# Softmax over rows of 512: the last chunk's last row loaded by GpSimd in two unequal DMAs

## The chip, the cores and the metric

One core of one Trainium2 chip. The metric is device time in microseconds (us), the median over executions. The kernel before takes 162.28 us (six runs, 162.11 to 162.43). The profiles are of single executions; their span is some 1.8 us shorter than the device time of the same execution.

## The reference

```python
x: (16, 1024, 512) float32
def reference(x):
    x_scaled = x / 0.5
    x_max = np.max(x_scaled, axis=-1, keepdims=True)
    exp_x = np.exp(x_scaled - x_max)
    return exp_x / np.sum(exp_x, axis=-1, keepdims=True)
```

The input has 33.55 MB, and so has the output. Everything has to cross the DMA engines once in each direction.

## The kernel before

The 16384 rows are cut into 8 chunks. A chunk is 128 partitions of 16 rows of 512 numbers, so 32 KB per partition and 4 MB in all. Six buffers hold the chunks; the seventh and eighth reuse the first two once these have been stored.

```python
    LOADS = [[(0, 4), (4, G)]] + [WHOLE] * 7
    BLOCKS = [[(0, 4), (4, 8), (8, G)]] + [WHOLE] * 6 + [[(0, 8), (8, G)]]
    STORES = [WHOLE] * 8
    BUFS = 6
# ...
        for lo, hi in LOADS[c]:                       # SyncE issues all loads
            nc.sync.dma_start(out=xt[:, lo:hi, :], in_=xr[c][:, lo:hi, :])
# ...
    # per block: maxima (VectorE), exponentials with row sums (ScalarE),
    # reciprocal and multiplication of 7 rows in 8 (VectorE), the rest (ScalarE), store
        nc.vector.tensor_reduce(negmax[:, 0:b], chunks[c][:, lo:hi, :], axis=AX, op=MAX, negate=True)
# ...
            nc.scalar.activation(out=row, in_=row, func=EXP, bias=biases[i][:, g : g + 1],
                                 scale=2.0, accum_out=sums[i][:, g : g + 1])
# ...
        nc.vector.tensor_mul(rows, rows, recips[i][:, 0:k].unsqueeze(2).broadcast_to((P, k, D)))
# ...
                nc.scalar.dma_start(out=outr[c][:, lo:hi, :], in_=chunks[c][:, lo:hi, :])
```

Of the kernel before, what the change touches and what calls it, by code (L numbers as in the profile page):

```python
# [1 line left out]

# [4 lines left out]


@with_exitstack
def kernel(  # L10
    ctx: ExitStack,
    tc: tile.TileContext,
    x: bass.AP,
    out: bass.AP,
):
    nc = tc.nc
    fp32 = mybir.dt.float32
    P = nc.NUM_PARTITIONS
    AX = mybir.AxisListType.X
    EXP = mybir.ActivationFunctionType.Exp  # L20
    COPY = mybir.ActivationFunctionType.Copy
    MAX = mybir.AluOpType.max

    D = x.shape[-1]
    xf = x.flatten_outer_dims()
    of = out.flatten_outer_dims()
    N = xf.shape[0]




    G = 16
    C = N // (P * G)
    assert C * P * G == N
    xr = xf.rearrange("(c p g) d -> c p g d", p=P, g=G)
    outr = of.rearrange("(c p g) d -> c p g d", p=P, g=G)
    WHOLE = [(0, G)]
    LOADS = [[(0, 4), (4, G)]] + [WHOLE] * 7
    BLOCKS = [[(0, 4), (4, 8), (8, G)]] + [WHOLE] * 6 + [[(0, 8), (8, G)]]
    STORES = [WHOLE] * 8  # L40
    BMAX = 16
    BUFS = 6

    data = ctx.enter_context(tc.tile_pool(name="data", bufs=BUFS))
    stats = ctx.enter_context(tc.tile_pool(name="stats", bufs=6))

    ctx.enter_context(tc.manual_schedule())


    warm = stats.tile([P, 1], fp32, name="warm", bufs=1)  # L50
    nc.vector.memset(warm, 0.0)  # L51
    nc.scalar.activation(out=warm, in_=warm, func=EXP)  # L52

    chunks = {}
    blocks = [(c, lo, hi) for c in range(C) for lo, hi in BLOCKS[c]]
    n = len(blocks)
    biases, sums, recips = {}, {}, {}

    def load(c):
        if c < BUFS:  # L60
            chunks[c] = data.tile([P, G, D], fp32, name="xt")
        else:
            chunks[c] = chunks[c - BUFS]
        xt = chunks[c]
        for lo, hi in LOADS[c]:
            nc.sync.dma_start(out=xt[:, lo:hi, :], in_=xr[c][:, lo:hi, :])  # L66

    def shift(i):
        c, lo, hi = blocks[i]
        if c not in chunks:  # L70
            load(c)
        b = hi - lo
        negmax = stats.tile([P, BMAX], fp32, name="negmax")
        nc.vector.tensor_reduce(  # L74
            negmax[:, 0:b], chunks[c][:, lo:hi, :], axis=AX, op=MAX, negate=True
        )
        biases[i] = stats.tile([P, BMAX], fp32, name="bias")
        nc.vector.tensor_scalar_mul(biases[i][:, 0:b], negmax[:, 0:b], 2.0)  # L78

    def exponentials(i, rows):  # L80
        c, lo, hi = blocks[i]
        if i not in sums:
            sums[i] = stats.tile([P, BMAX], fp32, name="sums")
        for g in rows:
            row = chunks[c][:, lo + g, :]
            nc.scalar.activation(  # L86
                out=row,
                in_=row,
                func=EXP,
                bias=biases[i][:, g : g + 1],  # L90
                scale=2.0,
                accum_out=sums[i][:, g : g + 1],
            )


    def scale_vector(i):
        c, lo, hi = blocks[i]
        b = hi - lo
        k = b - b // 8
        recips[i] = stats.tile([P, BMAX], fp32, name="recip")  # L100
        nc.vector.reciprocal(recips[i][:, 0:b], sums[i][:, 0:b])  # L101
        rows = chunks[c][:, lo : lo + k, :]
        nc.vector.tensor_mul(  # L103
            rows, rows, recips[i][:, 0:k].unsqueeze(2).broadcast_to((P, k, D))
        )

    def scale_scalar(i):
        c, lo, hi = blocks[i]
        b = hi - lo
        for g in range(b - b // 8, b):  # L110
            row = chunks[c][:, lo + g, :]
            nc.scalar.activation(  # L112
                out=row, in_=row, func=COPY, scale=recips[i][:, g : g + 1]
            )

    def store(i):
        c, _, end = blocks[i]
        for lo, hi in STORES[c]:
            if hi == end:
                nc.scalar.dma_start(  # L120
                    out=outr[c][:, lo:hi, :], in_=chunks[c][:, lo:hi, :]
                )

    shift(0)
    shift(1)

    def rows(i):
        c, lo, hi = blocks[i]
        cut = hi - lo - (2 if c == 1 else 0)
        return range(cut), range(cut, hi - lo)  # L130

    exponentials(0, rows(0)[0])
    for i in range(n):
        if i + 1 < n:
            exponentials(i + 1, rows(i + 1)[0])
        scale_vector(i)
        scale_scalar(i)
        if i + 2 < n:
            shift(i + 2)
        store(i)  # L140
        if i + 1 < n:
            exponentials(i + 1, rows(i + 1)[1])


# [1 line left out]
_INS = ['x']  # L146
_OUTS = [((16, 1024, 512), 'float32')]


# [23 lines left out]
```

## Time and profile before

A DMA is cut into packets, which sixteen DMA engines carry. When an engine is through with its share, it writes a completion count of 4 B to the DMA's semaphore, a counter; a DMA has landed when all sixteen have written.

| what | kernel before | from |
|---|---|---|
| device time | 162.28 us | median of six runs |
| span of the profiled execution | 160.26 us | profile |
| VectorE busy | 134.6 us, idle after 147.42 | page; chain of work |
| bytes moved | 67.13 MB, 431 GB/s from 2.5 to 148 us | transfers view |
| last data packet ends | 159.06 us, the other engines' by 158.51 | packet records |
| last completion count of the last store | 159.41 us | completion records |
| from that count to the end of the span ("the tail") | 0.85 us | difference |

The page's third part splits the transfers by queue. The columns are packets, megabytes, and the time of these packets as a share of sixteen engines' span:

```profile
q1 hardware_dynamic: 1296, 33.56, 49.4%
q10 hardware_dynamic: 1152, 33.55, 48.5%
q14 instruction: 2, 0.02, 0.0%
```

q1 has the loads, q10 the stores, q14 the fetches of instructions. Loads and stores together hold the engines for 97.9% of the span.

### The profile page before, as it was taken

The page shows a single profiled execution, that of the slowest core. Times are in us where ns is not written, and L with a number is a line of the kernel's source. Part 1 is how long each engine was busy: PE and PEld are TensorE (multiplying, and loading weights), DVE is VectorE, ACT ScalarE, POOL GpSimd, SP SyncE. Part 2 cuts the span into 40 slices and gives each one's busy share as a digit, 9 for nine tenths or more (in the row PEclk, how much of TensorE's full clock was granted, in tenths as well). Part 3 has the DMA queues.
Part 4 walks back from the last instruction along what each step waited for, and adds up shares of the span by engine and source line. Part 5 has one row for each costly group of instructions (what it writes and reads, how often), then busy time and mean ns, then how long its engine had stood idle before and what let it go on. Part 6 is the DMA issues. An engine that isn't in the chain of part 4 may idle for free.

```text
span 160.3 us, 402 instructions
## 1 busy us (share of the span) xinstructions
DVE 134.6 (84%) x45; ACT 102.2 (64%) x273; POOL 0.2 (0%) x4
## 2 busy tenths in 40 slices
DVE  0607999999999999999999999999999999957000
ACT  3071549069989972998199909991899891690000
POOL 0000000000000000000000000000000000000000
DMA  5999999999999999999999999999999999999993
GB/s 180 474 409 491 409 401 483 425 393 452 458 393 401 393 425 474 409 393 499 417 393 474 442 393 468 442 393 442 474 393 417 491 401 401 491 417 401 466 442 139
DMA packets 2450, 67.13 MB, mean 419 GB/s; under 512 B 272, under 2 KB 272, under 8 KB 272
## 3 DMA queue, kind: packets, MB, share of 16 engines
q1 hardware_dynamic: 1296, 33.56, 49.4%
q10 hardware_dynamic: 1152, 33.55, 48.5%
q14 instruction: 2, 0.02, 0.0%
HBM read 33.55 MB, written 33.55 MB: 419 GB/s over the span
## 4 chain that ended last, share of the span: by engine, by line
DVE 80%; DMA 7%; ACT 4%; issue 0%; SPq 0%
DVE negmax L74 42%; DVE xt L103 36%; DMA xt<-in_x_dram 7%; ACT xt L86 4%; DVE bias L78 1%; DVE recip L101 1%; SPq L66 0%
## 5 line engine op out<-in xcount | busy, mean ns | idle before, releaser
L86 ACT ACTIVATE xt<-xt,bias 128x512 f32<-128x512 f32 x128 | 90.4, 708 | 41.5 <-DVE bias L78 40.6
L74 DVE TENSOR_REDUCE negmax<-xt 128x16 f32<-128x8192 f32 (+2 forms) x11 | 69.9, 6353 | 9.5 <-DMA xt<-in_x_dram 9.5
L103 DVE TENSOR_TENSOR xt<-xt,recip 128x7168 f32<-128x7168 f32 (+2 forms) x11 | 62.0, 5637 | 0.4
L86 ACT ACTIVATION_READ_ACCUMULATOR xt<-xt,bias 128x1 f32 x128 | 23.9, 187 | 0.0
L112 ACT ACTIVATE xt<-xt,recip 128x512 f32<-128x512 f32 x15 | 9.9, 707 | 0.0
L101 DVE RECIPROCAL recip<-sums 128x16 f32<-128x16 f32 (+2 forms) x11 | 2.4, 218 | 1.8 <-ACT xt L86 1.8
L78 DVE TENSOR_SCALAR bias<-negmax 128x16 f32<-128x16 f32 (+2 forms) x11 | 1.9, 173 | 0.4
L52 ACT ACT_TABLE_LOAD x1 | 1.3, 1283 | 0.7 <-PEq L157 0.7
L51 DVE MEMSET warm<- 128x1 f32 x1 | 0.1, 59 | 0.8 <-PEq L157 0.8
L52 ACT ACTIVATE warm<-warm 128x1 f32<-128x1 f32 x1 | 0.2, 202 | 0.0
L157 POOL MEMSET const-bfloat16-1.0<- 128x1 bf16 x1 | 0.1, 101 | 0.0
L157 POOL MEMSET const-uint8-127<- 128x1 uint8 x1 | 0.1, 101 | 0.0
L157 POOL MEMSET const-float32-0.0<- 128x1 f32 x1 | 0.1, 98 | 0.2 <-issue 0.2
L157 POOL MEMSET const-float32-1.0<- 128x1 f32 x1 | 0.1, 98 | 0.0
## 6 DMA issues: line engine op xcount, KB each, us to landing
out_dram<-xt ACTq DMA_DIRECT2D x8, 4096.0 KB, 22.8
xt<-in_x_dram SPq DMA_DIRECT2D x7, 4096.0 KB, 30.1
xt<-in_x_dram SPq DMA_DIRECT2D x1, 3072.0 KB, 11.7
xt<-in_x_dram SPq DMA_DIRECT2D x1, 1024.0 KB, 4.8
```

What stands on the lines that cost most here:

```text
L51: nc.vector.memset(warm, 0.0)
L52: nc.scalar.activation(out=warm, in_=warm, func=EXP)
L74: nc.vector.tensor_reduce(negmax[:, 0:b], chunks[c][:, lo:hi, :], axis=AX, op=MAX, negate=True)
L78: nc.vector.tensor_scalar_mul(biases[i][:, 0:b], negmax[:, 0:b], 2.0)
L86: nc.scalar.activation(out=row, in_=row, func=EXP, bias=biases[i][:, g : g + 1], scale=2.0, accum_out=sums[i][:, g : g + 1],)
L101: nc.vector.reciprocal(recips[i][:, 0:b], sums[i][:, 0:b])
L103: nc.vector.tensor_mul(rows, rows, recips[i][:, 0:k].unsqueeze(2).broadcast_to((P, k, D)))
L112: nc.scalar.activation(out=row, in_=row, func=COPY, scale=recips[i][:, g : g + 1])
L157: nc = _bacc.Bacc("TRN2", target_bir_lowering=False, num_devices=1)
```

## The change

The last row of the last chunk is taken out of SyncE's load. GpSimd loads it in two DMAs: two partitions first, then the other 126. It starts when the sixth chunk's eleventh exponential is done, which it sees by copying that exponential's sum. The row is cut into halves of 1 KB. The intent, as far as the code shows it, is to give sixteen DMA engines unequal shares: one partition each for two of them, nine each for fourteen.

```diff
-    LOADS = [[(0, 4), (4, G)]] + [WHOLE] * 7
+    LOADS = [[(0, 4), (4, G)]] + [WHOLE] * 6 + [[(0, G - 1)]]
...
+    def load_last_row(signal):
+        seen = stats.tile([P, 1], fp32, name="seen", bufs=1)
+        nc.gpsimd.tensor_copy(out=seen, in_=signal)
+        c = C - 1
+        halves = "p (h d) -> p h d"
+        to = chunks[c - BUFS][:, G - 1, :].rearrange(halves, h=2)
+        of_ = xr[c][:, G - 1, :].rearrange(halves, h=2)
+        for p0, p1 in ((P - 2, P), (0, P - 2)):
+            nc.gpsimd.dma_start(
+                out=to[p0:p1], in_=of_[p0:p1], max_dma_last_dim=2 * D
+            )
...
+            if c == BUFS - 1 and g == 10:
+                load_last_row(sums[i][:, g : g + 1])
```

## The prediction

> **What bounds the kernel now.** I read the page first, then the chain of work, then the transfers view in narrow stretches, and at last the single transfer packets of the trace.
>
> The page shows two candidates, VectorE and the DMA engines:
>
> ```profile
> DVE 134.6 (84%) x45; ACT 102.2 (64%) x273; POOL 0.2 (0%) x4
> ...
> DVE  0607999999999999999999999999999999957000
> ...
> DMA  5999999999999999999999999999999999999993
> ...
> HBM read 33.55 MB, written 33.55 MB: 419 GB/s over the span
> ```
>
> VectorE is full from slice 5 to slice 35 and then has nothing; the DMA engines are full from slice 1 to the last. So the end belongs to the transfers, although the page's chain of work gives VectorE 80%. That chain stops at VectorE's last multiplication, as its last lines say:
>
> ```profile
> 137.51 5.76 ACT xt L86 x16
> 143.27 0.02 issue
> 143.29 0.21 DVE recip L101
> 143.51 0.02 issue
> 143.53 3.89 DVE xt L103
> ```
>
> VectorE is done at 143.53 + 3.89 = 147.42 us and the last store is issued at 147.50, but the span is 160.3. Whether those 12.8 us began late because of VectorE is seen in the packets: the store before it still has packets until 148.37 to 148.83 on fifteen engines and 149.37 on one, and each engine starts its first packet of the last store 6 ns after the completion write of the store before. The engines never ran dry, so VectorE has some 0.9 us to spare at the end, and only what sits on a DMA engine counts. The transfers view over 2.5 to 148 us says the same: 431 GB/s with no hole.
>
> Not all sixteen engines end together. The transfers view of 157.31 to 158.11 us counts packets that start there:
>
> ```profile
> DMA packets 1, 0.03 MB, mean 41 GB/s; under 512 B 0, under 2 KB 0, under 8 KB 0
> ```
>
> Fifteen engines had begun their last 32 KB packet by 157.30 us; one begins it at 157.84. A 32 KB packet takes 1213 ns, so the fifteen end between 158.12 and 158.51 and the straggler at 159.06; the completion counts agree (fifteen by 158.89, the sixteenth at 159.41). Why is one late? Two packets in the whole span are not data. The transfers view of 37.4 to 37.6 us, and that of 96.7 to 96.8, each have this kind of line:
>
> ```profile
> q14 instruction: 1, 0.01, 9.7%
> ```
>
> They are fetches of instructions, 8192 B and 309 ns each, at 37.51 and 96.79 us. The trace names no engine, but packets can be strung into sixteen chains, because the next packet of an engine starts 3 to 6 ns before the last one's end. Both fetches fall into one chain, and it is the one that ends at 159.06. 2 x 309 = 618 ns explains its lag of 545 ns on the next. So the last 0.5 us of this kernel is one DMA engine that has fetched instructions.
>
> **What the Trainium skill says.** "Runtime: NRT & Kernel Launch", section "Instruction fetch mechanics": the sequencer drives its own DMA queue to fetch the next page of instructions. The trace agrees that such fetches ride on the data engines; it shows packets of 8 KB where the page speaks of blocks of 16 KiB. "DMA: Bandwidth & Descriptors", section "Why a DMA increments its semaphore by 16 and not by 1": the number of engines is the largest up to 16 that divides the slowest dimension, and for GpSimd's DMAs with fewer than 16 they are consecutive engines from a round-robin cursor. It names an exception in which GpSimd's direct copies go to 16 engines with the partitions rounded up. No transfer before is GpSimd's, so the trace can't decide. The same page, "SWDGE vs HWDGE vs iDMA": GpSimd writes these descriptors into rings in SBUF, and all issuers share the same 16 engines. "SBUF — State Buffer", section "Who interferes with whom": a two-input VectorE instruction contends with GpSimd's reads, a reduction never does on trn2.
>
> **The change, part by part.** It is not meant to make anything faster, only to take bytes off the straggler. If the cursor starts at 0, two partitions go to engines 0 and 1, one each, and 126 = 14 x 9 go to engines 2 to 15, nine each; 2 + 14 = 16 also leaves the cursor where it was. I read the intent as: the fetching engine is one of the first two.
>
> Removed: the sixteenth row of the last load, 128 partitions x 2 KB, eight partitions or 16 KB per engine. Cost of bytes: 8192 B take 309 ns and 32768 B 1213 ns, and each follows the last about 4 ns early, so 904 ns for 24 KB = 37.7 ns per KB and about 4 ns fixed. 16 KB x 37.7 = 0.60 us off every engine (the packet count there stays, 30 KB in place of 32).
>
> Added on two engines: one partition, two pieces of 1 KB (the row is cut in halves): 2 x (37.7 + 4) = 0.08 us, if a piece has its own fixed part of 4 ns; up to 0.11 if it is some 15. Net -0.50 us for the straggler: 159.06 - 0.50 = 158.56.
>
> Added on fourteen: nine partitions, 18 pieces: 18 x 41.7 = 0.75 us to 18 x 53 = 0.95. Net +0.15 to +0.35: the last of them goes from 158.51 to 158.66 to 158.86. So these become the ones that end last, and the end moves from 159.06 to about 158.76: -0.30 us. The best that could be got by taking the whole lag away is 0.55.
>
> Off the path: GpSimd's copy of one column and the two descriptor runs. The eleventh exponential of the sixth chunk is done at about 104.0 us (the ACT instruction that starts at 103.25 plus its accumulator read), and VectorE's reduction starts at 103.88 and runs 8.68 us, so the descriptors are written beside a reduction. The buffer's earlier store landed at 87.4, so GpSimd waits for the exponential alone. VectorE needs the row at 132.86, over 25 us later. VectorE's and ScalarE's instruction order does not change; the comparison of the two builds shows only GpSimd's copy and two DMAs more, and a shorter last load. Sum: 162.35 - 0.30 = 162.05; I take 162.1 for the chance that it misses.
>
> **The rivals.** First, **the light share falls on other engines**, because the cursor is elsewhere, the fetching engine is not among the first two, or the exception applies. Then the straggler gets 8 or 9 partitions in small pieces: up to +0.35 us, 162.5 to 162.7. For it: nothing in the profile names engines. Against it: an odd pair first and 126 after, summing to 16 engines, makes no sense unless somebody knew which engine is late. I give it a quarter.
>
> Second, **GpSimd's small packets cost more than their bytes**, since the engines have to read descriptors out of SBUF first, or share turns among three rings. For it: no such transfer in this trace, so the 4 to 15 ns are only a guess from large packets. If a piece costs 80 ns instead of 45, the fourteen gain 18 x 35 = 0.6 us more and the end goes to 162.7. Against it: 126 x 2 pieces are 0.25 MB of 67.
>
> Third, **VectorE becomes the bound**: if GpSimd's work held it up by over 0.9 us, the last store would start late. One copy of 128x1 elements can't do that, and the stretch was chosen beside a reduction; 5%. Fourth, **the whole is hidden in the noise**: the three runs before span 162.11 to 162.43, as wide as the gain. That is the likely look of the result at three runs.
>
> **Range and chances.** Working as meant gives 161.95 to 162.15; the two rivals 162.5 to 162.7; with run-to-run spread of 0.15 the range is 161.8 to 162.7. Two per cent would be 3.2 us, six times the whole lag to be won, so faster by that has 0.01; slower by that needs a stall of GpSimd's path of over 3 us on an engine, 0.02; the same 0.97.
>
> **What would show it.** Right: fifteen or more engines end within 0.3 us, the lone late packet is gone from the end, 252 + 4 packets of GpSimd's queue appear at 104 to 110 us, VectorE's chain is unmoved to 0.1 us, and the last completion count comes at 158.9 to 159.2 in place of 159.41. Wrong: the lone late packet is still there (mapping), or all engines end 0.5 us later together (small packets), or the first packet of the last store waits for its issue (VectorE). A time outside 161.8 to 162.7 would mean a cost that I have not seen.

## More of the kernel before

The waits of SyncE's queue (line, what it waited for, us in total, times, longest) tell how the kernel ends, since SyncE looks through all completion semaphores before the core may stop. L168 is the end of the program:

```profile
SPq L168 <- DMA out_dram<-xt: 71.4, 4, 28.9
```

There are four such waits, one after another as the stores land. What comes after the last of them is the tail.

## The result, and the profile after

The changed kernel takes 162.14 us (median of six, 162.05 to 162.24) against 162.28. The ratio is 0.9993, with a 95% interval of 0.998 to 1.0006. A ratio here is the mean time of one kernel's runs over that of the other's of the same rounds, so it is not quite the ratio of the two medians. The time lies in the predicted range, and the difference is not clear of noise.

The page of the changed kernel, first the busy times, then VectorE's and the transfers' busy tenths, then the queues:

```profile
DVE 134.6 (84%) x45; ACT 102.2 (64%) x273; POOL 1.9 (1%) x7
...
DVE  0608999999999999999999999999999999957000
...
DMA  5999999999999999999999989999999999999993
...
q1 hardware_dynamic: 1296, 33.29, 49.1%
q10 hardware_dynamic: 1152, 33.55, 48.5%
q0 software_dynamic: 128, 0.26, 0.4%
q14 instruction: 2, 0.02, 0.0%
HBM read 33.55 MB, written 33.55 MB: 419 GB/s over the span
```

VectorE and ScalarE do what they did. q0 is GpSimd's queue; it has taken 0.26 MB over from q1. Of its 128 packets, 56 of 4096 B and 16 of 2048 B have the data: the 1 KB pieces were put together. The other 56 are completion counts and fillers of 16 B at most. The two fetches are still there.

The end of the chain of work (start, length, what) shows VectorE 0.09 us earlier than before. That comes from the start of the program (the second load landed at 12.71 us in place of 12.80) and is no effect of the change:

```profile
143.20 0.21 DVE recip L120
143.42 0.02 issue
143.44 3.89 DVE xt L122
```

The transfers view of 157.31 to 158.11 us, the stretch in which the kernel before had one lone packet:

```profile
DMA packets 7, 0.20 MB, mean 246 GB/s; under 512 B 1, under 2 KB 1, under 8 KB 1
```

and of 157.6 to 158.2 us:

```profile
DMA packets 1, 0.00 MB, mean 0 GB/s; under 512 B 1, under 2 KB 1, under 8 KB 1
```

Six engines now begin their last 32 KB packet after 157.31, and none after 157.6; the one packet in the second line is a completion count of 4 B. In this profile the lone late engine has joined the field. In the repeat of the same kernel ("again", below) it hasn't quite; its view of 157.6 to 158.2 us has one 32 KB packet of that engine besides a count:

```profile
DMA packets 2, 0.03 MB, mean 55 GB/s; under 512 B 1, under 2 KB 1, under 8 KB 1
```

The packets strung into chains (as in the prediction) say it in full for the first profile: the engine with the two fetches got one packet of 2048 B from q0 and ends at 158.77; another engine that got 2048 B ends first, at 158.01; the fourteen with 18 KB end between 158.31 and 158.67. The last packet ends 0.29 us earlier than before.

Yet the span is 160.27 us, where it was 160.26. So the gain of 0.29 was given back between the last packet and the end. The completion count came at 159.15 in place of 159.41, a gain of 0.26. From there to the end of the span ("the tail") it takes 1.12 us in place of 0.85. The waits of SyncE's queue show what has become of the end:

```profile
SPq L187 <- DMA out_dram<-xt: 43.5, 1, 43.5
SPq L187 <- DMA xt<-in_x_dram: 27.8, 1, 27.8
```

SyncE now stands at one single wait for 43.5 us, until the very last store has landed, and everything else that it has to look at comes after it. The page doesn't count semaphore instructions; the trace has them. Each of SyncE's waits looks at two semaphores. Eight semaphores (100 and 102 to 108) serve the DMAs of SyncE and ScalarE in turn, and the last store, the seventeenth, counts on the first of them, 100:

| after the last count, us | before | changed |
|---|---|---|
| SyncE then looks at | 108 and VectorE's; ScalarE's | 105 and 111; 106 and 110; 107 and VectorE's; 108 and ScalarE's; GpSimd's |
| SyncE signals that it is through | 0.180 | 0.365 |
| end of the span | 0.854 | 1.122 |

110 and 111 are the semaphores of the two GpSimd DMAs. They make the list longer, and the list's new order puts semaphore 100 ahead of more of it. Three waits more at 60 ns each are 0.185 us. The remaining 0.083 us is after that: GpSimd's drain takes 103 ns in place of 70, its clearing of the semaphores 138 in place of 93. Together 0.27 us, against 0.26 won.

GpSimd's own work, as the timeline of its engine has it (start, length, instruction, idle time before it):

```profile
104.03 0.18 POOL L87 COPY seen<-sums 128x1 f32<-128x1 f32 x1 [103.58 <-ACT xt L103]
104.76 1.48 POOL L93 DMA_DIRECT2D xt<-in_x_dram  x2 [0.55 <-issue]
```

and the DMA issues (what, queue, KB each, us from issue to landing):

```profile
xt<-in_x_dram POOLq DMA_DIRECT2D x1, 252.0 KB, 15.2
xt<-in_x_dram POOLq DMA_DIRECT2D x1, 4.0 KB, 8.7
```

The row is there at 120.7 us, 12 us before VectorE needs it. Slow as the transfer is, nobody waits for it.

### The profile page after: what moved, and what is told of

Read it like the earlier page. It is cut to its first block, busy times and chain, and to the rows that moved or that the text cites. A ratio compares the mean times of both kernels' runs of the same rounds, so it can differ in the third digit from the quotient of the medians. Undisturbed runs are those within 1.5% of the kernel's fastest.

```text
span 160.3 us, 410 instructions
## 1 busy us (share of the span) xinstructions
DVE 134.6 (84%) x45; ACT 102.2 (64%) x273; POOL 1.9 (1%) x7
## 4 chain that ended last, share of the span: by engine, by line
DVE 75%; DMA 7%; issue 5%; ACT 3%; SPq 0%
DVE negmax L74 42%; DVE xt L122 32%; DMA xt<-in_x_dram 7%; ACT xt L103 3%; DVE bias L78 1%; DVE recip L120 1%; SPq L66 0%
## 5 line engine op out<-in xcount | busy, mean ns | idle before, releaser
L93 POOL DMA_DIRECT2D xt<-in_x_dram x2 | 1.5, 741 | 0.5 <-issue 0.5
```

Source lines behind the costliest of these rows:

```text
L93: nc.gpsimd.dma_start(out=to[p0:p1], in_=of_[p0:p1], max_dma_last_dim=2 * D)
```

## The experiments

The theory: (1) the engine that fetches instructions is the last, and the change takes 14 KB off it; (2) that gain is eaten by a longer tail; (3) VectorE's chain, which the page puts at 80% of the span before and 75% after, does not set the end. The rivals: the gain does not depend on which engine gets the light share; the tail's growth is chance; VectorE's chain sets the end. A fourth, that the late engine is slow of itself and not by its fetches, no run tests; the packets of the profiles settle it (see the point on the bound, below). All runs gave correct results. "Last packet", "last count" and "tail" are from the run's one profile, the ratio from five or six timed runs against the kernel before.

| run | last packet | last count | tail | ratio | 95% interval |
|---|---|---|---|---|---|
| before | 159.06 | 159.41 | 0.85 | 1 | |
| changed | 158.77 | 159.15 | 1.12 | 0.9993 | 0.998 to 1.0006 |
| again | 158.96 | 159.31 | 1.12 | 0.9991 | 0.9978 to 1.0003 |
| tiny | 159.27 | 159.62 | 1.13 | 1.0019 | 1.0006 to 1.0033 |
| swap | 159.31 | 159.68 | 1.13 | 1.0029 | 1.0016 to 1.0041 |
| whole | 159.17 | 159.52 | 1.05 | 1.0010 | 0.9997 to 1.0022 |
| early | 158.91 | 159.27 | 1.13 | 0.9990 | 0.9974 to 1.0006 |
| late | 158.74 | 159.11 | 1.13 | 1.0003 | 0.9987 to 1.0019 |
| late2 | 159.33 | 159.69 | 1.12 | 1.0020 | 1.0008 to 1.0032 |
| lanes2_before | 159.41 | 159.77 | 0.82 | 0.9995 | 0.9982 to 1.0007 |
| lanes2_after | 158.81 | 159.26 | 0.90 | 0.9978 | 0.9966 to 0.9991 |
| two_rows | 159.28 | 159.76 | 1.12 | 0.9986 | 0.9973 to 1.0000 |

### again: the changed kernel once more

No edit.

> The changed kernel once more, unedited. Theory: the engine that fetches instructions got one partition instead of eight, so its last packet ends some 0.3 us earlier than before the change (158.7 to 158.9 us in place of 159.06), but SyncE then steps through three more waits of 60 ns and the clearing of semaphores is 45 ns longer, so span and time end within 0.2 us of the kernel before: ratio 0.998 to 1.001. Rival: the first profile was a chance draw, and either the packet's end or the tail (last landing to span's end, 1.12 us there against 0.85 before) comes out elsewhere by over 0.15 us.

The tail is 1.12 us again, the time ratio 0.9991. The last packet ends at 158.96, 0.19 us later than in the first profile. That is over the 158.7 to 158.9 expected and over the 0.15 us that the rival asked for. But the second load had landed 0.19 us later too (12.90 us against 12.71): counted from there, both profiles have their last packet at 146.06 us, where the kernel before has 146.26. So the tail repeats to the hundredth, and here the end of the packets moved with the start of the program. A single profile is good for the tail and only fair for the packets' times on the clock.

### tiny: all of the machinery, none of the shift

```diff
-    LOADS = ... + [WHOLE] * 6 + [[(0, G - 1)]]
+    LOADS = ... + [WHOLE] * 7
...
-        for p0, p1 in ((P - 2, P), (0, P - 2)):
-            nc.gpsimd.dma_start(out=to[p0:p1], ...)
+        for k in range(2):          # 16 partitions x 8 bytes, never read
+            nc.gpsimd.dma_start(out=scrap[0:16, 2*k : 2*k+2], in_=xr[0][0:16, 0, 2*k : 2*k+2])
```

> The kernel before, its last load whole, plus GpSimd's copy of the signal and two GpSimd DMAs of 128 bytes each that nobody reads: all of the change's machinery without its shift of bytes. Theory (the machinery costs 0.26 us in the tail): last landing as before at 159.4, tail 1.12 in place of 0.85, time 0.2 to 0.35 us over the kernel before (ratio 1.0012 to 1.002). Rival (the tail's growth has another cause, or is hidden): tail 0.85, ratio 1.000.

The tail is 1.13 us with the same list of waits as in the changed kernel, and the time is up by 0.19% or 0.31 us (0.0019 x 162.3), clear of noise. The last count came at 159.62, not at the 159.4 expected. The machinery costs that by itself. In the same rounds the changed kernel with the shift ("again") has 0.9991, so the shift of bytes is worth 0.0028 x 162.3 = 0.45 us. In these rounds that is the whole result: 0.45 won, 0.31 paid. The interval of each ratio is 0.2 us to either side, so the sizes are rough; the tail, 0.28 us longer in the profile, is the firmer figure of what is paid.

### swap: the 126 partitions first

```diff
-        for p0, p1 in ((P - 2, P), (0, P - 2)):
+        for p0, p1 in ((0, P - 2), (P - 2, P)):
```

> The changed kernel with its two GpSimd DMAs in the other order: 126 partitions first, then two. Theory (a cursor deals engines in turn, so the light share now falls on the last two of the sixteen): the fetching engine gets nine partitions, its last packet ends 0.1 to 0.25 us later than before the change (159.15 to 159.3), last landing near 159.6, time 0.3 to 0.6 us over the kernel before. Rival (the place of the light share doesn't hang on the order): like the changed kernel, last packet 158.8.

The transfers view of 157.6 to 158.2 us has the lone late packet back:

```profile
DMA packets 1, 0.03 MB, mean 55 GB/s; under 512 B 0, under 2 KB 0, under 8 KB 0
```

It is the 32 KB packet of one engine alone, and in the chains this engine has the two fetches and now 18432 B from GpSimd's queue. It ends at 159.31, at the upper edge of what was expected; the next at 158.61. The time is 0.29% up, 0.38% or 0.6 us over "again" in the same rounds, for the same instructions in another order. The difference in bytes on that engine is 16 KB; the packets of GpSimd's queue took 159 ns per 4096 B, so 4 x 155 ns = 0.62 us. The place of the light share decides, and it does hang on the order of the two DMAs.

### whole: one DMA of all 128 partitions

```diff
-        for p0, p1 in ((P - 2, P), (0, P - 2)):
+        for p0, p1 in ((0, P),):
```

> The changed kernel with one GpSimd DMA of all 128 partitions, so eight per engine. Theory: the fetching engine keeps its lag of some 0.5 us on the others and ends at 159.05 to 159.2; one semaphore fewer than the changed kernel, so the tail is 1.0 to 1.1 us; time 0.2 to 0.4 us over the kernel before. Rival (moving a row to GpSimd's queue helps by itself, whatever engine it lands on): last packet at 158.8 as in the changed kernel.

The last packet is a lone one again and ends at 159.17, in the range expected. The tail is 1.05 us, one semaphore shorter than the changed kernel's. The time is 0.10% up, 0.16 us, a little less than the 0.2 to 0.4 expected and not clear of zero. Moving a row to GpSimd's queue has no merit of its own.

### lanes_before and lanes_after: the last store on another semaphore, first try

```diff
                 nc.scalar.dma_start(out=outr[c][:, lo:hi, :], ...)
+        if c == 5:
+            for k in range(7):      # 16 partitions x 4 bytes, never read
+                nc.sync.dma_start(out=scrap7[0:16, k : k+1], in_=xr[0][0:16, 0, k : k+1])
```

Seven DMAs more make twenty-four, three times around the eight semaphores, so the last store counts on the eighth, which SyncE looks at nearly last.

> The kernel before plus seven loads of 64 bytes by SyncE in mid-kernel that nobody reads, so that the last store counts on the eighth completion semaphore, not on the first, and SyncE looks at it nearly last. Theory: from last landing to the span's end 0.75 to 0.85 us (0.85 before; at most one wait of 60 ns fewer), the tiny loads cost under 0.1 us, time within 0.15 us of the kernel before.

> The changed kernel plus the same seven loads of 64 bytes. Theory (three waits of 60 ns stand behind the last store's semaphore in the final waits): the tail from last landing to the span's end falls from 1.12 to some 0.9 us and the time to 0.25 to 0.4 us below the kernel before (ratio 0.9975 to 0.9985). Rival (the tail's growth is GpSimd's own, in its drain and the clearing of semaphores): tail stays 1.05 to 1.12 and the time is that of the changed kernel.

The tails came as the theory has them: 0.81 and 0.90 us. The times did not: ratios of 1.0362 and 1.0331, 5.9 and 5.4 us slower, which was not expected. The cause is the edit itself. With seven DMAs between two stores, the fourth store got the semaphore of the third, which was still in flight, and had to wait for it. ScalarE's waits in "lanes_before" (line, for what, us in total, times, longest):

```profile
ACT xt L86 <- DMA out_dram<-xt: 15.4, 1, 15.4
```

A store that would have been issued at 92.2 us was issued at 107.15, and ScalarE's next exponential waited behind it for the 15.4 us of the line above. As times, these two runs say nothing of the tail.

### lanes2_after and lanes2_before: the same, mended

```diff
                 nc.scalar.dma_start(out=outr[c][:, lo:hi, :], ...)
+        for k in range({5: 4, 6: 3}.get(c, 0)):   # 16 partitions x 4 bytes, never read
+            scrap = stats.tile([P, 1], fp32, name="scrap", bufs=7)
+            nc.sync.dma_start(out=scrap[0:16], in_=sums[i][0:16, k : k + 1])
```

Four wait for the sixth chunk's sums and three for the seventh's, so no store follows its predecessor on the same semaphore.

> The changed kernel plus seven copies of 64 bytes inside SBUF by SyncE, four that wait for the sixth chunk's sums and three for the seventh's, so that the last store again counts on the eighth completion semaphore, but no store shares one with the store right before it. Theory (final waits): the stores are issued as in the changed kernel (last one at 147.4 to 147.6), tail 0.9 us in place of 1.12, time 0.25 to 0.45 us below the kernel before (ratio 0.997 to 0.9985) and 0.15 to 0.25 below the changed kernel. Rival (the tail saved is lost again elsewhere, as the seven copies sit on the engines): time that of the changed kernel, ratio 0.999.

> The kernel before plus the same seven copies. Theory: tail 0.81 us in place of 0.85 (one wait fewer), last packet at 159.05 to 159.2, time within 0.15 us of the kernel before (ratio 0.9990 to 1.001). If it were as much below the kernel before as the changed kernel with copies is, the semaphore's place alone would be the gain and the shift of bytes nothing.

The stores are issued as before, the last at 147.43 in "lanes2_after" and 147.41 in "lanes2_before". SyncE's waits for stores at the end of the program, in "lanes2_after":

```profile
SPq L190 <- DMA out_dram<-xt: 37.8, 4, 9.7
```

Four waits again, each store as it lands, and 0.90 us of tail in place of 1.12. The time is 162.02 us against 162.45 of the kernel before on that chip, ratio 0.9978, and the whole interval is under 1. "lanes2_before", in the same rounds, has 0.9995: the semaphore's place alone makes no clear difference to the kernel before, whose tail had but one wait to lose (0.82 in place of 0.85). (Its last packet, at 159.41, was later than the 159.05 to 159.2 expected.) So the shift of bytes is worth 0.0017 x 162.3 = 0.28 us here, with the tail's growth nearly gone (0.08 us are left of it); the 0.45 us of "tiny" and this agree within their intervals. The version beats the kernel before by 0.22%, clear of noise. It was not timed beside the changed kernel; its ratio is 0.0013 to 0.0015 below (0.21 to 0.24 us), which is what the tail lost (0.22 us), but the intervals overlap. What the tail lost is shown by the profile; that the time fell by as much is likely, not shown.

### early: the signal from the second exponential

```diff
-            if c == BUFS - 1 and g == 10:
+            if c == BUFS - 1 and g == 1:
```

> The changed kernel with the signal taken from the second exponential of the sixth chunk in place of the eleventh: GpSimd writes its descriptors some 6 us earlier, beside VectorE's two-input multiplication. Theory (the moment does not matter, the row has 25 us to spare and only bytes per engine count): last packet 158.7 to 158.9, time within 0.1 us of the changed kernel. Rival (GpSimd and VectorE hold each other up there): GpSimd's DMA instructions take several us in place of 1.5, or VectorE's multiplication 7.63 us grows, and the last store is issued later than 147.5.

The time is that of the changed kernel. GpSimd's timeline, however, is not:

```profile
97.72 6.24 POOL L87 COPY seen<-sums 128x1 f32<-128x1 f32 x1 [97.28 <-ACT xt L103]
103.91 1.48 POOL L93 DMA_DIRECT2D xt<-in_x_dram  x2
```

and VectorE's in the same stretch:

```profile
96.30 7.62 DVE L122 TENSOR_TENSOR xt<-xt,recip 128x7168 f32<-128x7168 f32 x1
103.84 8.68 DVE L74 TENSOR_REDUCE negmax<-xt 128x16 f32<-128x8192 f32 x1
```

The copy of one column that took 0.18 us now takes 6.24 and ends when VectorE's multiplication ends. This is the contention that the prediction speaks of, a two-input instruction against GpSimd's read; beside the reduction the same copy took 0.18 us. VectorE isn't held up (7.62 us as ever), and the DMAs go out no earlier than 103.91, only 0.85 us ahead of the changed kernel's. The rival was right about the contention and wrong about what it costs: nothing, as nobody waits. It also shows why the eleventh exponential is a sensible signal: it comes when the reduction starts.

### late and late2: VectorE's chain made longer

```diff
+        if i == n - 1:
+            idle = stats.tile([P, 480], fp32, name="idle", bufs=1)   # late2: 1100
+            nc.vector.memset(idle, 0.0)
         nc.vector.tensor_mul(
```

> The changed kernel with a VectorE memset of 128x480 right before its last multiplication, some 0.55 us, so that the last store is issued that much later (148.0 in place of 147.42). Theory (the engines still hold the store before when it arrives; a store's first packet starts 0.84 us after its issue, so 148.8 against engines free at 148.6 to 149.1): the last packet ends 0 to 0.15 us later, time within 0.15 us. Rival (VectorE's chain sets the end, as the page's chain of work has it): everything 0.5 to 0.6 us later.

The multiplication started 0.37 us after where it would have, and the store was issued at 147.84, not at 148.0. The last packet ended at 158.74. The profile is for the theory; the time ratio of 1.0003 is some 0.2 us above that of "early" (0.9990) in the same rounds, with an interval of 0.16% on either side, and alone would leave it open. Hence a stronger dose:

> The changed kernel with a memset of 128x1100 before VectorE's last multiplication (that of 128x480 took 0.46 us, of which 0.37 delayed the multiplication), so that the last store is issued some 1.0 us later, at 148.4 to 148.6. Theory (a store's first packet starts 0.84 us after its issue, so 149.3 to 149.45, and the engines are through with the store before at 148.0 to 149.1): only what the engines now wait counts, 0.2 to 0.4 us for the last of them; last packet at 158.95 to 159.25, time 0.1 to 0.45 us over the changed kernel. Rival (VectorE's chain sets the end): time 1.0 us over it, last packet at 159.8.

The timeline of "late2" around the last store:

```profile
143.79 0.97 DVE L124 MEMSET idle<- 128x1100 f32 x1 [0.18 <-issue]
144.68 3.83 DVE L125 TENSOR_TENSOR xt<-xt,recip 128x3584 f32<-128x3584 f32 x1
148.59 0.34 ACTq L142 DMA_DIRECT2D out_dram<-xt  x1
```

The transfers view of 157.3 to 158.5 us:

```profile
DMA packets 16, 0.52 MB, mean 437 GB/s; under 512 B 0, under 2 KB 0, under 8 KB 0
```

The store is issued 1.0 to 1.17 us later than in "again" and the first profile (147.60 and 147.42). All sixteen engines had run dry by then and begin the store together, the first packet at 149.44, 0.845 us after the issue; all sixteen begin their last packet in that one stretch. The last ends at 159.33, at the upper side of what was expected (158.95 to 159.25 and a little over). The time is 0.29% above "again" (another set of rounds), 0.47 us, where VectorE's chain as the bound would have cost 1.0 us or more. So some 0.6 us of delay was free.

### two_rows: twice the dose

```diff
-    LOADS = ... + [[(0, G - 1)]]
+    LOADS = ... + [[(0, G - 2)]]
...
-        to = chunks[c - BUFS][:, G - 1, :].rearrange("p (h d) -> p h d", h=2)
+        to = chunks[c - BUFS][:, G - 2 : G, :].rearrange("p g (h d) -> p (g h) d", h=2)
```

(and the same for the source)

> The changed kernel with the last two rows of the last chunk loaded by GpSimd in the same two DMAs, so the light engines lose 28 KB and the other fourteen gain 4. Theory (the fourteen become the bound, and each row costs them 0.15 us net): the fetching engine ends at 158.3 to 158.5, the last of the fourteen at 158.75 to 158.95, so the end is that of the changed kernel or up to 0.15 us later; time ratio 0.999 to 1.000. Rival (more taken off the late engine is more won): last packet at 158.5, time 0.3 us below the changed kernel.

The profiled execution was the slowest of its five (162.66 us, the others 162.13 to 162.23), so its end is not that of a usual run. In its chains the engine with the fetches ends between 158.38 and 158.48 (the packets can be strung in several ways here), as expected, and twelve of the fourteen end between 158.36 and 158.61; the other two, however, end at 159.07 and 159.28. The last of these has packets of 1216 to 1241 ns in many places where 1213 is usual. Why, the trace does not tell. The time, 0.9986 and so a little under the 0.999 to 1.000 expected, is neither the 0.3 us gain over the changed kernel that the rival asked for (some 0.9973) nor told apart from the changed kernel's. The dose makes no clear difference; more than that this run can't say.

## Why the prediction was right or wrong, point by point

**The bound: right, but a fetch costs twice what was reckoned.** The DMA engines own the end, and of them the one with the two fetches. "swap", "tiny" and "whole" leave it its bytes, and a lone packet ends last at 159.17 to 159.31; the runs that relieve it (changed, again, early, late, lanes2_after) end at 158.74 to 158.96. Within one profile, where no common start is needed, the last engine of the first kind of run (before, tiny, swap, whole, lanes2_before) ends 0.77 to 0.95 us after the median of the other fifteen, that of the second kind 0.23 to 0.44. "late2" shows that VectorE is not the bound.

Nor is that engine slow of itself. In the chains of the kernel before, its completion counts come 0.16 us ahead of the median of the others up to the first fetch, and 0.51 us behind right after it. That is 0.67 us, where the fetch took 0.31: the packet that follows it took 1578 ns in place of 1213 (1575 to 1584 in all runs of the table). After the second fetch it was 1459 in place of 1213, or 1382 to 1384 in place of 1138 where the packet has 30 KB. So the two fetches cost 309 + 365 + 309 + 246 ns = 1.23 us. "2 x 309 = 618 ns explains its lag of 545 ns on the next" is therefore a wrong reading: it sets the bare packets against the lag on the slowest of the others, and the lag on their median is 0.81 us. Why the packet after a fetch takes longer, the trace does not tell.

**VectorE's "some 0.9 us to spare": wrong in its working.** I set the issue of the last store at 147.50 against the first free engine at 148.37. A store's first packet starts 0.84 us after its issue (0.840 in the changed kernel, where one light engine stood idle for 0.215 us; 0.845 in "late2"). So the store could start at 148.34, and the first free engine had some 0.03 us to spare, the last of the fifteen 0.49, the late one 1.03. "late2" put what the kernel as a whole can bear at some 0.6 us. Beyond that the engines would be waiting for VectorE.

**The mapping: right.** Two and 126 partitions gave two engines one partition each and fourteen nine each, and one of the two is the engine with the fetches. The first rival had a quarter of the chances; "swap" shows what it would have looked like, 0.29% slower.

**The size on the fourteen: too high.** The pieces of 1 KB did not stay single. Four packets of 4096 B at 155 ns and one of 2048 B at 80 ns are 0.70 us, not 0.75 to 0.95; against this stand eight packets that shrank from 1213 to 1138 ns, 0.60 us. So the fourteen gained 0.10 us, not 0.15 to 0.35. "These become the ones that end last" failed by a little: they ended by 158.67, the relieved engine at 158.77, and in all five relieved runs it was still the last, by 0.01 to 0.24 us.

**The size on the late engine: about right.** 80 ns for its 2 KB, some 40 ns for small filler packets (below), less 0.60, is -0.48; I had -0.50. The first profile shows only -0.29 for the end. The end of the packets scatters by 0.2 us and more: "again" differs from the first profile by 0.19 (its start was as much later), "lanes2_before" from the kernel before by 0.35. Over runs with and without relief, the mean last packet is at 158.84 (five relieved runs) against 159.23 (before, tiny, whole, lanes2_before), -0.39 us. My figure for the end, 158.76, was met at 158.77 in the first profile, with both parts of it somewhat off.

**The sum: the term that was missing.** "Sum: 162.35 - 0.30 = 162.05" ends at the last packet. The step "Off the path: GpSimd's copy of one column and the two descriptor runs" looked at when GpSimd works and not at what it leaves behind: two DMA semaphores and one of GpSimd's own, to be looked at and cleared when all is done. This measured 0.27 us in the tail and 0.31 us of time in "tiny". Measured change: -0.07% or -0.11 us, where the sum had -0.30. The time landed within 0.04 us of the 162.1 forecast by luck: the sum started from 162.35, the median of three runs, where six gave 162.28, and 0.05 us had been added for other risks; these two made up for most of the missing term. By its parts: -0.26 at the last count, +0.27 in the tail, 0.01 in the span of the profiled execution.

**The signs.** Two of those named for "right" came true: the last count at 159.15, and VectorE's chain moved by 0.09 us. The others did not come as written: fifteen engines end within 0.46 us, not 0.3; GpSimd's queue has 128 packets from 110.4 to 120.0 us, not 256 at 104 to 110; and the lone late packet is gone in the first profile, "late" and "lanes2_after" but not in "again" and "early". None of the signs looked past the last count, so none could show the tail.

**The rivals.** Small packets did not cost more than their bytes. GpSimd and VectorE met only in "early", where it was free. "Hidden in the noise" was the right look of the result at six runs, but for another reason than the one given: the effect (-0.11 us where -0.30 was summed) had first been cut to a third by the tail.

## What to carry to other kernels

In a kernel whose transfers never pause, look at each DMA engine's own end and not at the mean, since one engine that carries something extra is the end of all. Each DMA on a new queue also added a semaphore to the final waits, so count the time from the last landing to the end of the span before and after. Where the last store's semaphore is looked at early in that list, what stands behind it comes after the last landing; here its place in the list was worth 0.22 us of tail, against 0.26 us that the change had won at the last count of its first profile.

## What the Trainium skill lacked or had wrong

- "DMA: Bandwidth & Descriptors", "Why a DMA increments its semaphore by 16 and not by 1": the division by two and by 126 and the cursor agree with the trace (two engines with 2048 B, fourteen with 18432 B; the light share moved with the order of the DMAs alone). The exception for direct copies did not appear with this form. Lacking: an engine with no share of such a DMA takes a filler packet for each data packet of the others, four of 16 B and one of 8 B on each light engine and one of 8 B on each of the fourteen, 9 to 11 ns each; those of the light engines come one after every packet of the other queue. Lacking too is how long the start of a transfer takes on busy engines (the page's first-byte figures don't say at what load they hold): GpSimd's first DMA was issued at 104.76 us and had its first packet at 110.36, 5.6 us later; ScalarE's first store of the same profile, with nothing before it on its queue, was issued at 44.03 and had its first packet at 48.33, 4.3 us later; a store on an idle engine had it after 0.84 us. So most of GpSimd's 5.6 us may be the busy engines' and not its own.
- "Runtime: NRT & Kernel Launch", "Instruction fetch mechanics": it has refills of 16 KiB whose cost is mostly hidden. The trace has single packets of 8 KB, 59 us apart, both on one DMA engine. With full engines the cost is not hidden: 0.67 and 0.56 us a fetch, the longer packet after it included, and that engine ends 0.55 us after the rest.
- No page has the final waits of the program itself: SyncE looks at two semaphores at a time, some 60 ns for each pair. How much of the list comes after the last landing hung on which semaphore the last store had (tail 1.12 us against 0.90 with seven copies more); two GpSimd DMAs and a copy made the tail 1.12 us in place of 0.85.
